# A chunked encoder layer with a mixture of experts: adaLN scales of two chunks on VectorE, features of a chunk in three rounds, and the last expert's scatter block by block

## The chip, the cores and the metric

The kernel runs on one core of a Trainium2 chip. Times are microseconds (us) on the device, from the first to the last instruction of the program and the launch around it. TensorE appears in the profile as PE (its weight loads as PEld), VectorE as DVE, ScalarE as ACT, GpSimd as POOL; SyncE (SP) issues nearly all loads. What is measured is the median of several executions.

## The reference, cut to what matters

One layer, 256 tokens, width 2048, all in float32. Every matrix product of the mixer is done on TensorE as three products of a high and a low part.

```python
mod = c_act @ w_ada[l] + b_ada[l]                 # 2048 x 12288
sh1, sc1, g1, sh2, sc2, g2 = split(mod, 6)
h = rms_norm(x, g_mix[l]) * (1 + sc1) + sh1       # "scale" sc1 and "shift" sh1 of the mixer
y = token_mixer(h, w_in[l], ...)                  # z = h @ w_in, 2048 x 4616; gMLP, pooling, attention; @ w_out
x = x + g1 * y
h = rms_norm(x, g_ffn[l]) * (1 + sc2) + sh2
x = x + g2 * moe_ffn(h, ...)                      # router, 16 experts of 2048 x 1024, top 2 of one group of 4
```

## The kernel before

The program is one long hand-written order; no scheduler moves anything. `h @ w_in` is done in five **chunks** of features (`CHUNKS`: 256, 256, 512, 512, 512 of the 2048), called chunk 0 to chunk 4 here. A chunk's `h` needs its shift (section 0 of `w_ada`) and its scale (section 1), which are themselves sums over the 2048 rows of `w_ada`; they are computed while the chunk ahead is multiplied. Chunks 0 and 1 have small pieces, chunks 2 to 4 nine **pieces** of 512 columns each.

A piece is four steps. Each step's `prep` casts a 128 x 512 tile of weights to its high part on ScalarE (line 175) and subtracts to get the low part (line 176, `whl`) on the engine that `WSPLIT` names: for chunks 2 to 4 one step of four on VectorE and three on GpSimd. Its `run` issues six matmuls into two PSUM banks (`pm`). After the fourth step `put` (line 460) adds both banks into `z` on VectorE. There are three such banks, so a piece's second bank is the first bank of the piece ahead: its fourth matmul waits for the first of the two adds of `put`.

`step` keeps a queue, `todo`, of steps whose `prep` has been issued: new ones go in at one end, and `run_first` takes the oldest out when the weights in the queue exceed `LOOK`. `then` puts a small job in the same queue. So the order on every engine is fixed by this queue and by the strings in `PLAN`: an `n` there is one `w_ada` tile for the next chunk (four row blocks of 128 x 512), a digit joins a finished shift or scale to `mod`, `h` is `make_h` of the next chunk.

A `w_ada` tile is worked in one of two ways. `ada_parts` multiplies its four row blocks on TensorE (`ada<-ring,cact`); at the end the sums are copied by ScalarE (`r`, line 314) and transposed. `sum_parts` does the same on VectorE: four multiply-and-adds into a PSUM bank (`ada`, line 297), the last of the sixteen into `ga` in SBUF, which TensorE then sums over partitions with a column of ones (`pt<-ones,ga`). `M1A` and `M1B` choose, for the shift and the scale of chunks 1 to 4: "P" is TensorE, "V" VectorE. Before, the shifts of chunks 3 and 4 are on VectorE, and all scales on TensorE.

`make_h` makes the features of a chunk: for each 128 of them VectorE scales and shifts (`hf`, line 420), ScalarE casts the high part, VectorE subtracts the low part (`hT`, line 176), and only then the next 128 follow. Eight or four more matmuls (`lgp`) use `hf`.

After the mixer come `w_out`, the router, and 15 experts in the order `ORDER`. Each loads twelve tiles of 2 MB through a ring (`load`, line 1358) whose addresses come from registers that the router's result fills. `down_stage` makes four blocks of 512 output columns: matmuls (`lbank`), a multiply by the gate on VectorE (`y`), and `late`, the scatter of the block ahead: two matmuls (`bank<-y,gt`), two adds into `xa` (line 1350) and, for the last expert only, two stores of 256 KB on ScalarE's queue (`out_dram<-xa`). The last `late` of an expert is returned and run during the next expert's loads, or, for the last one, by `pend()`. Then every engine reads `n_ov`, the number of overflow rounds, into a register, and a loop over it follows that runs no round here.

Of the kernel before, what the change touches and what calls it, by code (L numbers as in the profile page):

```python
# [11 lines left out]
F32 = mybir.dt.float32  # L12
# [4 lines left out]
OP = mybir.AluOpType  # L17
# [5 lines left out]
KD = D // 128  # L23
# [21 lines left out]
ORDER = [9, 0, 3, 10, 1, 4, 11, 2, 5, 12, 6, 7, 13, 8, 14]  # L45
# [20 lines left out]

G2, G2_MID, NG2 = [1, 2, 1, 1], 1, 8

M1A, M1B, M2A, M2B, G1 = "PPVV", "PPPP", "PPPP", "PPPP", "PVVV"
WSPLIT, WSO = ["VGVG", "VGVG", "GVGG", "GVGG", "GVGG"], "GVGG"  # L70
NORM = "GV"

# [44 lines left out]
def body(tc, x_d, prm_d, bg_d, wada_d, win_d, wout_d, egu_d, ed_d, out_d):  # L117
# [31 lines left out]

    todo = deque()  # L150

    def run_first():
        f, x, _ = todo.popleft()
        f(x) if x is not None else f()

    def step(prep, run, split=False):
        todo.append((run, prep(), split))
        while sum(0 if x is None else 1 if p else 2 for _, x, p in todo) > LOOK:
            run_first()

    def then(f):
        todo.append((f, None, False)) if todo else f()

    def flush():
        while todo:
            run_first()

    V, S, G, E = nc.vector, nc.scalar, nc.gpsimd, nc.tensor

    def mm(out, lhsT, rhs, start=True, stop=True):  # L170
        E.matmul(out, lhsT=lhsT, rhs=rhs, start=start, stop=stop, skip_group_check=True)  # L171


    def split(hi, lo, src, eng=None):
        S.copy(hi, src)  # L175
        (eng or V).tensor_tensor(lo, src, hi.bitcast(F32), op=OP.subtract)  # L176
# [65 lines left out]
    def pt():  # L242
        tbanks.rotate(-1)
        return tbanks[-1]
# [3 lines left out]
    cact = cst.tile([128, KD], F32, name="cact")  # L248
# [3 lines left out]
    def ada_load(sec, k0, nk, g):  # L252
        n = 128 * nk
        w = ring()
        load_tile(w, wada_d, ADA[sec, k0, g])
        return w.rearrange("p (k n) -> p k n", n=n)
# [23 lines left out]
    def sum_parts(sec, k0, nk, after, acc, eng, tile_of, bias=None):  # L280
        r = 16 // nk
        ng = KD // r
        P = accs[acc][:, :128 * nk]
        buf = []

        def one(g):
            def prep():
                return ada_load(sec, k0, nk, g)

            def run(w):  # L290
                for j in range(r):
                    k = r * g + j
                    ck = cact[:, k:k + 1]
                    if k == 0:
                        eng.tensor_scalar(P, w[:, j, :], ck, None, op0=OP.mult)
                    elif k < KD - 1:
                        eng.scalar_tensor_tensor(P, w[:, j, :], ck, P, op0=OP.mult, op1=OP.add)
                    else:
                        a = tile_of()[:, :128 * nk]
                        eng.scalar_tensor_tensor(a, w[:, j, :], ck, P, op0=OP.mult, op1=OP.add)  # L300
                if g == ng - 1:
                    if bias is not None:
                        eng.scalar_tensor_tensor(a[0:8, :], bgt, ident[0:8, bias:bias + 1], a[0:8, :],
                                                 op0=OP.mult, op1=OP.add)
                    after(a)
            return prep, run
        return [one(g) for g in range(ng)]

# [88 lines left out]
    def hbuf(q):  # L397
        return hTs[(len(CHUNKS) - q) % 2]
# [8 lines left out]
    def make_h(q):  # L407
        k0, nk = CHUNKS[q]
        hq = hbuf(q)
        ts = []  # L410
        for c in range(nk):
            k = k0 + c
            if c % 2 == 0:
                p2 = pt()
                for j in range(4):
                    o = 128 * (c + j // 2)
                    E.transpose(p2[:, 128 * j:128 * j + 128], xn[:, j % 2, o:o + 128], ident)
            p = p2[:, 256 * (c % 2):256 * (c % 2) + 256]
            t = wk.tile([128, T], F32, name="hf", bufs=5)
            V.tensor_scalar(t, p[:, :T], mod[:, 1, k:k + 1], mod[:, 0, k:k + 1], op0=OP.mult, op1=OP.add)  # L420
            split(hq[:, 0, c, :], hq[:, 1, c, :], t)
            ts.append((k, t))

        def late():
            for k, t in ts:
                o = 32 * (k % 4)
                mm(fzp[o:o + 8, :], wfz[:, k, :], t, start=k < 4, stop=k >= KD - 4)
        todo.insert(6, (late, None, False)) if todo else late()
# [691 lines left out]
    for h in range(2):  # L1120
        V.tensor_scalar(oneh[:, h, :], io512, sl2[:, 0, h:h + 1], None, op0=OP.is_equal)
        V.scalar_tensor_tensor(oneh[:, h, :], io512, sl2[:, 1, h:h + 1], oneh[:, h, :].bitcast(F32),
                               op0=OP.is_equal, op1=OP.add)
# [80 lines left out]
    def wide():  # L1204
        wide_ring.rotate(-1)
        return wide_ring[-1]
# [114 lines left out]
    def down_stage(w, hid, gt, load, done=None):  # L1321


        nt = 128 // w
        lhs = hid_T(w, hid)
        late = None
        for b in range(4):
            P = lbank()
            c0 = 512 * b
            t = wide()  # L1330
            load(t, ed_d, b)
            v = t.rearrange("p (k n) -> p k n", k=8)
            for kk in range(8):
                j = kk % nt
                if w == 128:
                    hl = split_piece(v[:, kk, :])
                    mm3(P, *lhs(kk), hl[:, 0, :], hl[:, 1, :], kk == 0, kk == 7)
                    continue
                mm(P[w * j:w * j + w, :], lhs(kk), v[:, kk, :], start=kk < nt, stop=kk >= 8 - nt)
            y = mo.tile([128, 512], F32, name="y")  # L1340
            V.tensor_tensor(y, P, g2w[:, c0:c0 + 512], op=OP.mult)  # L1341
            if late is not None:
                late()

            def late(y=y, c0=c0):
                for h in range(2):
                    p = bank()
                    mm(p, gt[:, 128 * h:128 * h + 128], y)
                    a = xa[:, h, c0:c0 + 512]
                    V.tensor_tensor(a, a, p, op=OP.add)  # L1350
                    if done is not None:
                        done(h, c0)
        return late

    def make_load(e):
        def load(t, flat, i):
            n = 128 * 2 * RINGW
            nc.sync.dma_start(t, flat[ds(e, 1), n * i:n * i + n].rearrange("a (p m) -> p (a m)", p=128))
        return load

    def reg(i, engines, hi, why):
        return nc.values_load(irow[0:1, i:i + 1], engines=engines, min_val=0, max_val=hi,
                              skip_runtime_bounds_check_because=why)

    why = "computed on the chip within these bounds"
    pend = None
# [21 lines left out]
    xr = tokens(ORDER[0])  # L1388
    for i, r in enumerate(ORDER):
        w = CAPS[r]  # L1390
        load = make_load(reg(r, [SP], NE - 1, why))
        gts = []
        if pend is not None:
            fill.append(pend)
        fill.insert(1, lambda: gts.append(onehot_T(w, lambda h: posR[:, h, r:r + 1], lambda h: gatR[:, h, r:r + 1])))
        hid = up_stage(w, xr, load)
        if i + 1 < len(ORDER):
            xr = tokens(ORDER[i + 1])
        pend = down_stage(w, hid, gts[0], load, store if r == ORDER[-1] else None)
    pend()  # L1400


    n_ov = reg(48, list(mybir.ALL_ENGINES), 16, why)
    for s in (s_mo, s_psB, s_psL):
        s.close()
    with tc.For_i(0, n_ov, 1) as i, ExitStack() as inner:
        mo = inner.enter_context(tc.tile_pool(name="mo2", bufs=1))
        psL = inner.enter_context(tc.tile_pool(name="psL2", bufs=6, space=PSUM))
        psB = inner.enter_context(tc.tile_pool(name="psB2", bufs=2, space=PSUM))
        e = nc.values_load(irow[0:1, ds(i + 64, 1)], engines=[SP], min_val=0, max_val=NE - 1,  # L1410
                           skip_runtime_bounds_check_because=why)
        s0 = nc.values_load(irow[0:1, ds(i + 80, 1)], engines=[DVE], min_val=0, max_val=384,
                            skip_runtime_bounds_check_because=why)
        pg = mo.tile([128, 4], F32, name="pg")
        for h in range(2):
            V.tensor_copy(pg[:, h:h + 1], posO[:, h, ds(i, 1)])
            V.tensor_copy(pg[:, 2 + h:3 + h], gatO[:, h, ds(i, 1)])
        load = make_load(e)
        xr = tokens_of(128, s0)
        gt = onehot_T(128, lambda h: pg[:, h:h + 1], lambda h: pg[:, 2 + h:3 + h])  # L1420
        hid = up_stage(128, xr, load)
        down_stage(128, hid, gt, load, store)()

    for s in (s_pl, s_pg2, s_ring2, s_ring, s_cst, root):
        s.close()
# [43 lines left out]
```

## Time and profile before

| what | us |
|---|---|
| median of 3 executions (lowest, highest) | 1412.74 (1409.59, 1419.79) |
| the profiled execution's own time | 1414.28 |
| its span, first to last instruction | 1412.5 |
| PE busy | 1207.9 (86%) |
| DVE busy | 592.7 (42%) |
| ACT busy | 363.4 (26%) |
| POOL busy | 216.9 (15%) |

The shares are averages over stages with different limits: in the first third the engines wait for one another, in the last two thirds the DMA engines are never idle. So they are read only by stretch. In a timeline a row is a run of like instructions on one engine; what stands in brackets is how long that engine was idle ahead of the row and whose work it waited for.

### The profile page before, as it was taken

To read this page: it belongs to the slowest core of one execution; us is meant where nothing else is said; L and a number is where in the kernel's file an instruction comes from. 1 tells how busy PE (TensorE), PEld (TensorE's weight loads), DVE (VectorE), ACT (ScalarE), POOL (GpSimd) and SP (SyncE) were. 2 spreads that over 40 slices of the span, in tenths; PEclk is the share of its full clock that TensorE was granted. 3 is DMA by queue.
4 is the path that set the end of the run, shared out by engine and by line. 5 is a ranking of instruction groups with operands and counts; after the bars stand their busy time and mean duration, and the time that the engine had idled before them with its cause. 6 is when DMAs were issued, how large, how long until landed. Compare 5 with 4: busy or idle time off the path is not lost.

```text
span 1412.5 us, 17042 instructions
## 1 busy us (share of the span) xinstructions
PE 1207.9 (86%) x6646; PEld 627.1 (44%) x6646; DVE 592.7 (42%) x1121; ACT 363.4 (26%) x661; POOL 216.9 (15%) x170
## 2 busy tenths in 40 slices
PE   5989999999999887989869999688885888868865
PEld 2656766665676353763327643222232222322221
DVE  4356454655884735981238832122030221302112
ACT  4633434535443332860007720000000000000000
POOL 1335545422675000000000000000000000000000
PEclk9999999999999898999989999899997999969997
DMA  9887795899989789999999989999999999999996
GB/s 390 348 347 291 291 360 209 322 359 341 374 336 369 285 366 428 427 379 370 427 427 426 416 315 428 426 428 427 426 427 426 428 426 427 426 426 429 425 425 263
DMA packets 49222, 539.14 MB, mean 382 GB/s; under 512 B 5472, under 2 KB 5600, under 8 KB 7024
## 3 DMA queue, kind: packets, MB, share of 16 engines
q1 hardware_dynamic: 47664, 534.79, 92.4%
q10 hardware_dynamic: 1472, 3.19, 0.6%
q8 instruction: 55, 0.90, 0.3%
q14 instruction: 31, 0.25, 0.0%
HBM read 535.86 MB, written 2.10 MB: 381 GB/s over the span
## 4 chain that ended last, share of the span: by engine, by line
PE 51%; DMA 35%; issue 4%; DVE 4%; ACT 2%; POOL 2%; SPq 0%; DVEq 0%; POOLq 0%; ACTq 0%
PE lbank L171 23%; PE pm L171 16%; DMA ring<-in_e_down_dram 15%; DMA ring<-in_e_gu_dram 14%; PE ada L171 5%; PE bank L171 4%; DMA ringl<-in_e_down_dram 2%; POOL whl L176 2%; DMA ringl<-in_e_gu_dram 2%; PE pt L171 1%; DMA ringm<-in_e_gu_dram 1%; DMA ring<-in_w_ada_dram 1%; DVE el L176 0%; ACT whl L175 0%; DMA bgt<-in_bg_dram 0%
## 5 line engine op out<-in xcount | busy, mean ns | idle before, releaser
L171 PE MATMUL pm<-whl,hT 128*128 128x512 f32 x1056 | 281.3, 403 | 13.0 <-DVE whl L176 6.1
L171 PEld LDWEIGHTS pm<-whl,hT 128*128 128x128 f32 x1056 | 198.7, 192 | 79.2 <-issue 11.9
L171 PE MATMUL lbank<-ring,xr 128*32 128x256 f32 (+1 forms) x1216 | 155.8, 494 | 42.9 <-DMA ring<-in_e_gu_dram 42.3
L176 POOL TENSOR_TENSOR whl<-ring,whl 128x512 fp32r<-128x512 f32 x116 | 160.8, 1408 | 181.8 <-ACT whl L175 177.5
L171 PE MATMUL bank<-y,gt 128*128 128x512 f32 x240 | 118.9, 618 | 0.0
L171 PEld LDWEIGHTS lbank<-ring,xr 128*32 128x32 f32 (+1 forms) x1216 | 55.9, 127 | 136.6 <-issue 70.0
L1350 DVE TENSOR_TENSOR xa<-xa,bank 128x512 f32<-128x512 f32 x120 | 82.5, 688 | 72.5 <-PE bank L171 72.5
L175 ACT CAST whl<-ring 128x512 fp32r<-128x512 f32 x164 | 94.6, 621 | 59.8 <-PE pm L171 46.5
L171 PE MATMUL lbank<-ringl,xr 128*32 128x256 f32 (+1 forms) x608 | 80.9, 516 | 31.7 <-DMA ringl<-in_e_gu_dram 31.7
L171 PE MATMUL lbank<-ring,hidT 128*64 128x512 f32 (+1 forms) x416 | 83.6, 703 | 28.3 <-DVE hidT L1309 16.5
L1341 DVE TENSOR_TENSOR y<-lbank,g2w 128x512 f32<-128x512 f32 x60 | 41.5, 692 | 156.8 <-PE lbank L171 156.8
L171 PE MATMUL lbank<-ringm,xr 128*32 128x256 f32 (+1 forms) x608 | 81.8, 520 | 21.2 <-DMA ringm<-in_e_gu_dram 21.2
L171 PE MATMUL lbank<-el,xs 128*128 128x512 f32 x384 | 91.1, 395 | 6.2 <-ACT el L175 4.1
L1291 DVE TENSOR_TENSOR hid<-hid,lbank 128x512 f32<-128x512 f32 x11 | 7.6, 688 | 202.4 <-PE lbank L171 202.2
L1237 ACT COPY gt<-bank 128x256 f32<-128x256 f32 x15 | 5.6, 372 | 337.1 <-PE bank L1235 337.1
L171 PEld LDWEIGHTS lbank<-el,xs 128*128 128x128 f32 x384 | 71.3, 188 | 26.1 <-ACT el L175 6.3
L460 DVE TENSOR_TENSOR z<-z,pm 128x512 f32<-128x512 f32 x72 | 49.1, 688 | 71.3 <-PE pm L171 71.1
L171 PE MATMUL lbank<-ringl,hidT 128*64 128x512 f32 (+1 forms) x416 | 74.2, 598 | 4.6 <-DMA ringl<-in_e_down_dram 4.6
L171 PE MATMUL ada<-ring,cact 128*1 128x512 f32 (+1 forms) x536 | 63.8, 575 | 16.3 <-DMA ring<-in_w_ada_dram 13.1
L171 PEld LDWEIGHTS bank<-y,gt 128*128 128x128 f32 x240 | 41.6, 191 | 72.7 <-issue 70.3
L1286 DVE TENSOR_TENSOR hid<-hid,lbank 128x256 f32<-128x256 f32 x6 | 2.5, 422 | 163.2 <-PE lbank L171 139.4
L175 ACT CAST el<-ring 128x512 fp32r<-128x512 f32 x96 | 57.4, 622 | 50.0 <-DMA ring<-in_e_gu_dram 42.9
(391 smaller groups left out, 1234.3 us busy)
## 6 DMA issues: line engine op xcount, KB each, us to landing
ring<-in_e_gu_dram SPq DMA_DIRECT2D x60, 2048.0 KB, 24.6
ring<-in_w_ada_dram SPq DMA_DIRECT2D x81, 1024.0 KB, 7.2
ringm<-in_e_gu_dram SPq DMA_DIRECT2D x30, 2048.0 KB, 25.4
ringl<-in_e_gu_dram SPq DMA_DIRECT2D x30, 2048.0 KB, 25.0
ring<-in_e_down_dram SPq DMA_DIRECT2D x30, 2048.0 KB, 25.3
ringl<-in_e_down_dram SPq DMA_DIRECT2D x30, 2048.0 KB, 25.7
ring<-in_w_in_dram SPq DMA_DIRECT2D x28, 1024.0 KB, 6.9
ring<-in_w_out_dram SPq DMA_DIRECT2D x12, 1024.0 KB, 8.4
```

The source lines that it names most:

```text
L171: E.matmul(out, lhsT=lhsT, rhs=rhs, start=start, stop=stop, skip_group_check=True)
L175: S.copy(hi, src)
L176: (eng or V).tensor_tensor(lo, src, hi.bitcast(F32), op=OP.subtract)
L460: V.tensor_tensor(dst, dst, P[h], op=OP.add)
L1237: S.copy(gt, p[:, :256])
L1286: V.tensor_tensor(hid[:, :256], hid[:, :256], P[1][:, :256], op=OP.mult)
L1291: V.tensor_tensor(hid[:, o], hid[:, o], P[2 * b + 1], op=OP.mult)
L1341: V.tensor_tensor(y, P, g2w[:, c0:c0 + 512], op=OP.mult)
L1350: V.tensor_tensor(a, a, p, op=OP.add)
```

## The change

Four edits. **Scales on VectorE**: `M1B` becomes "PPVV", so that the scales of chunks 3 and 4 (worked during chunks 2 and 3) go the way of the shifts. **Sums in twos**: a tile's first two multiply-and-adds are issued at its turn, the other two go into a second queue, `rest`, which is emptied after the next step's matmuls or ahead of the next job that is no step. **Three rounds**: `make_h` issues all `hf` of a chunk, then all casts, then all subtractions. **Last expert**: `late` of each block follows its own `y` at once, and `n_ov` is read ahead of the last expert.

```diff
-M1A, M1B, M2A, M2B, G1 = "PPVV", "PPPP", "PPPP", "PPPP", "PVVV"
+M1A, M1B, M2A, M2B, G1 = "PPVV", "PPVV", "PPPP", "PPPP", "PVVV"
...
+    rest = deque()
+
     def run_first():
-        f, x, _ = todo.popleft()
+        f, x, is_split = todo.popleft()
+        if not is_split:
+            drain()
         f(x) if x is not None else f()
+        if is_split:
+            drain()
+
+    def drain():
+        while rest:
+            rest.popleft()()
...
             def run(w):
                 for j in range(r):
...
+                    if 2 * j < r:
+                        add(w[:, j, :], r * g + j)
+                    else:
+                        rest.append(lambda wj=w[:, j, :], k=r * g + j: add(wj, k))
...
             V.tensor_scalar(t, p[:, :T], mod[:, 1, k:k + 1], mod[:, 0, k:k + 1], op0=OP.mult, op1=OP.add)
-            split(hq[:, 0, c, :], hq[:, 1, c, :], t)
             ts.append((k, t))
+        for c in range(nk):
+            S.copy(hq[:, 0, c, :], ts[c][1])
+        for c in range(nk):
+            V.tensor_tensor(hq[:, 1, c, :], ts[c][1], hq[:, 0, c, :].bitcast(F32), op=OP.subtract)
...
                     if done is not None:
                         done(h, c0)
+
+            if done is not None:
+                late()
+                late = None
         return late
...
+        if r == ORDER[-1]:
+            n_ov = reg(48, list(mybir.ALL_ENGINES), 16, why)
...
-    pend()
-
-
-    n_ov = reg(48, list(mybir.ALL_ENGINES), 16, why)
```

VectorE's rows at the entry of chunk 2, `make_h` between the scale's `mod` and the `put` of the last piece of chunk 1. Before:

```order
L342 SCALAR_TENSOR_TENSOR mod<-mod,prm_69 128x4
L420 TENSOR_SCALAR hf<-pt_122,mod 128x256
L176 TENSOR_TENSOR hT_133<-hf,hT_133 128x256
L420 TENSOR_SCALAR hf<-pt_122,mod 128x256
L176 TENSOR_TENSOR hT_133<-hf,hT_133 128x256
L420 TENSOR_SCALAR hf<-pt_123,mod 128x256
L176 TENSOR_TENSOR hT_133<-hf,hT_133 128x256
L420 TENSOR_SCALAR hf<-pt_123,mod 128x256
L176 TENSOR_TENSOR hT_133<-hf,hT_133 128x256
L460 TENSOR_TENSOR z<-z,pm_120 128x512
L460 TENSOR_TENSOR z<-z,pm_121 128x512
```

Now, on the same engine at the same place:

```order
L362 SCALAR_TENSOR_TENSOR mod<-mod,prm_69 128x4
L440 TENSOR_SCALAR hf<-pt_122,mod 128x256 x2
L440 TENSOR_SCALAR hf<-pt_123,mod 128x256 x2
L445 TENSOR_TENSOR hT_133<-hf,hT_133 128x256 x4
L483 TENSOR_TENSOR z<-z,pm_120 128x512
L483 TENSOR_TENSOR z<-z,pm_121 128x512
```

The four `hf` no longer alternate with the four subtractions that wait for ScalarE's casts.

VectorE's rows in the middle of chunk 2, from the last tiles of the shift (`spare_141`, `ring_63`) on; `whl` is a step's low part, `ring_64` and `ring_65` hold scale tiles where `cact` stands beside them. Before:

```order
L297 SCALAR_TENSOR_TENSOR ada_113<-spare_141,cact,ada_113 128x512 x4
L176 TENSOR_TENSOR whl<-ring_63,whl 128x512
L297 SCALAR_TENSOR_TENSOR ada_113<-ring_63,cact,ada_113 128x512 x3
L300 SCALAR_TENSOR_TENSOR ga<-ring_63,cact,ada_113 128x512
L460 TENSOR_TENSOR z<-z,pm_119 128x512
L460 TENSOR_TENSOR z<-z,pm_120 128x512
L176 TENSOR_TENSOR whl<-ring_65,whl 128x512
L176 TENSOR_TENSOR whl<-spare_140,whl 128x512
L460 TENSOR_TENSOR z<-z,pm_121 128x512
L460 TENSOR_TENSOR z<-z,pm_119 128x512
L337 TENSOR_TENSOR mod<-pt_122,prm_69 128x4
```

Now, on the same engine at the same place:

```order
L311 SCALAR_TENSOR_TENSOR ada_113<-spare_141,cact,ada_113 128x512 x2
L192 TENSOR_TENSOR whl<-ring_63,whl 128x512
L311 SCALAR_TENSOR_TENSOR ada_113<-spare_141,cact,ada_113 128x512 x2
L311 SCALAR_TENSOR_TENSOR ada_113<-ring_63,cact,ada_113 128x512 x3
L314 SCALAR_TENSOR_TENSOR ga<-ring_63,cact,ada_113 128x512
L483 TENSOR_TENSOR z<-z,pm_119 128x512
L483 TENSOR_TENSOR z<-z,pm_120 128x512
L309 TENSOR_SCALAR ada_113<-ring_64,cact 128x512
L311 SCALAR_TENSOR_TENSOR ada_113<-ring_64,cact,ada_113 128x512
L192 TENSOR_TENSOR whl<-ring_65,whl 128x512
L311 SCALAR_TENSOR_TENSOR ada_113<-ring_64,cact,ada_113 128x512 x6
L192 TENSOR_TENSOR whl<-spare_140,whl 128x512
```

The first `whl` moves two sums earlier; two sums of the scale stand ahead of the second, and six between the second and the third (the row of six takes in those of the next tile).

TensorE's rows at the end, from the last expert's first output block on. Before:

```order
L171 MATMUL lbank<-ring_63,hidT 32x512 x8
L171 MATMUL lbank<-ring_64,hidT 32x512 x8
L171 MATMUL bank<-y,gt 128x512 x2
L171 MATMUL lbank<-ringl_3884,hidT 32x512 x8
L171 MATMUL bank<-y,gt 128x512 x2
L171 MATMUL lbank<-ringl_3885,hidT 32x512 x8
L171 MATMUL bank<-y,gt 128x512 x4
L1362 TENSOR_LOAD irow
L1406 COMPARE_AND_BRANCH
```

Now, on the same engine at the same place:

```order
L187 MATMUL lbank<-ring_63,hidT 32x512 x8
L187 MATMUL bank<-y,gt 128x512 x2
L187 MATMUL lbank<-ring_64,hidT 32x512 x8
L187 MATMUL bank<-y,gt 128x512 x2
L187 MATMUL lbank<-ringl_3878,hidT 32x512 x8
L187 MATMUL bank<-y,gt 128x512 x2
L187 MATMUL lbank<-ringl_3879,hidT 32x512 x8
L187 MATMUL bank<-y,gt 128x512 x2
L1433 COMPARE_AND_BRANCH
```

Two scatter matmuls instead of four follow the last block, and the register load (`TENSOR_LOAD irow`) is gone from there.

## Rows read from the trace of the kernel before

**Rows 1.** Stretches: PE, PEld, DVE, ACT, POOL busy, granted clock, DMA share, GB/s.

```profile
100.00:150.00 50.00, 45.05 (x207) 32.88 (x208) 27.16 (x41) 19.30 (x33) 26.52 (x20) 0.93 0.75 291
...
900.00:1000.00 100.00, 82.83 (x378) 25.76 (x372) 21.36 (x40) 1.72 (x4) 0.00 (x0) 0.97 1.01 426
```

**Rows 2.** Chain of waits in order of time: start, us, what; features of chunk 0.

```profile
22.74 0.56 DVE hf L420
...
23.75 0.43 DVE hT L176
24.18 0.47 DVE hf L420
24.67 0.41 ACT hT L175
25.07 0.53 ACT whl L175
```

**Rows 3.** Timeline of TensorE at the entries of chunks 1 and 2.

```profile
61.37 3.69 PE L171 MATMUL pm<-whl,hT 128*128 128x512 f32 x15 [1.17 <-ACT z L458]
...
102.35 6.29 PE L171 MATMUL pm<-whl,hT 128*128 128x512 f32 x15 [3.40 <-DVE z L460]
```

**Rows 4.** Timeline of VectorE at the entry of chunk 2, first and last row.

```profile
96.21 0.54 DVE L420 TENSOR_SCALAR hf<-pt,mod 128x256 f32<-128x256 f32 x1
...
101.62 1.28 DVE L460 TENSOR_TENSOR z<-z,pm 128x512 f32<-128x512 f32 x2
```

**Rows 5.** Busy time of the first microseconds of chunk 2, columns as in rows 1.

```profile
102.00:105.00 3.00, 2.65 (x6) 2.15 (x7) 1.67 (x3) 1.43 (x3) 3.00 (x3) 0.50 0.32 57
```

**Rows 6.** Timeline of VectorE in the middle of chunk 2.

```profile
121.02 1.37 DVE L460 TENSOR_TENSOR z<-z,pm 128x512 f32<-128x512 f32 x2 [1.03 <-PE pm L171]
122.31 3.12 DVE L297 SCALAR_TENSOR_TENSOR ada<-spare,cact,ada 128x512 f32<-128x512 f32 x4
125.34 0.68 DVE L176 TENSOR_TENSOR whl<-ring,whl 128x512 fp32r<-128x512 f32 x1
125.94 2.33 DVE L297 SCALAR_TENSOR_TENSOR ada<-ring,cact,ada 128x512 f32<-128x512 f32 x3
```

**Rows 7.** Timeline of TensorE in chunks 2 and 3 and at the entries of chunks 3 and 4.

```profile
126.08 3.93 PE L171 MATMUL pm<-whl,hT 128*128 128x512 f32 x16 [2.60 <-DVE whl L176]
129.94 1.90 PE L171 MATMUL ada<-ring,cact 128*1 128x512 f32 x16
...
138.44 1.05 PE L171 MATMUL pt<-ones,ga 128*128 128x1 f32 x8
...
152.59 0.66 PE L327 MATMUL pt<-ident,r 128*128 128x128 f32 x4
...
188.63 5.56 PE L171 MATMUL pm<-whl,hT 128*128 128x512 f32 x16 [2.60 <-DVE whl L176]
...
230.97 7.00 PE L171 MATMUL pm<-whl,hT 128*128 128x512 f32 x28 [0.63 <-POOL whl L176]
```

**Rows 8.** Timeline of TensorE at the entry of chunk 3.

```profile
166.35 4.04 PE L171 MATMUL pm<-whl,hT 128*128 128x512 f32 x15 [0.24 <-POOL whl L176]
```

**Rows 9.** Timeline of the last expert's output.

```profile
1387.07 2.84 PE L171 MATMUL lbank<-ring,hidT 128*32 128x512 f32 x16 [2.97 <-DMA ring<-in_e_down_dram]
...
1392.45 11.54 ACTq L1319 DMA_DIRECT2D out_dram<-xa  x8
...
1397.15 1.93 PE L171 MATMUL lbank<-ringl,hidT 128*32 128x512 f32 x16 [0.83 <-DMA ringl<-in_e_down_dram]
...
1399.01 3.89 PE L171 MATMUL bank<-y,gt 128*128 128x512 f32 x8
...
1399.14 0.69 DVE L1341 TENSOR_TENSOR y<-lbank,g2w 128x512 f32<-128x512 f32 x1 [2.10 <-PE lbank L171]
```

**Rows 10.** Instructions of the register read and of the loop's branches, TensorE's queue.

```profile
L1362 PEldq TENSOR_LOAD <-irow x1: 703/703/703, 1401.8 to 1401.8; - x1
...
L1406 PEldq COMPARE_BRANCH  x3: 97/310/4230, 1402.7 to 1411.3; - x3
```

More of the change, by code (lines that the diff above doesn't have):

```diff
@@ L161, in then @@
     def then(f):
-        todo.append((f, None, False)) if todo else f()
+        if todo:
+            todo.append((f, None, False))
+        else:
+            drain()
+            f()
     def flush():
@@ L166, in flush @@
             run_first()
+        drain()
     V, S, G, E = nc.vector, nc.scalar, nc.gpsimd, nc.tensor
@@ L288, in prep, with add @@
                 return ada_load(sec, k0, nk, g)
[L290 to L301, printed above, removed]
+            def add(wj, k):
+                ck = cact[:, k:k + 1]
+                if k == 0:
+                    eng.tensor_scalar(P, wj, ck, None, op0=OP.mult)
+                elif k < KD - 1:
+                    eng.scalar_tensor_tensor(P, wj, ck, P, op0=OP.mult, op1=OP.add)
+                else:
+                    a = tile_of()[:, :128 * nk]
+                    eng.scalar_tensor_tensor(a, wj, ck, P, op0=OP.mult, op1=OP.add)
                     if bias is not None:
@@ L305, in run @@
                     after(a)
+            def run(w):
+                for j in range(r):
+                    if 2 * j < r:
+                        add(w[:, j, :], r * g + j)
+                    else:
+                        rest.append(lambda wj=w[:, j, :], k=r * g + j: add(wj, k))
             return prep, run
@@ L1421, in body @@
         hid = up_stage(128, xr, load)
-        down_stage(128, hid, gt, load, store)()
+        down_stage(128, hid, gt, load, store)
     for s in (s_pl, s_pg2, s_ring2, s_ring, s_cst, root):
```

## The prediction

> **What bounds the kernel now.** I read the stretches first. Up to the router TensorE is nearly full and the DMA engines are not; behind it the weights of the experts fill the DMA engines, at 426 GB/s, whatever TensorE does [rows 1]. The experts' loads cannot start before the router has given their addresses, so what is won ahead of it moves the whole stream forward, and the full amount arrives at the end. Three of the four edits lie ahead of it, the last expert's at its end.
>
> Inside the first part I read the chain of waits, then the timelines for TensorE's gaps. The chain runs through the features of a chunk one by one [rows 2]; TensorE stands still at every entry of a chunk [rows 3, 7, 8], longest, 3.40 us, ahead of chunk 2, and it waits 2.60 us for one `whl` of VectorE in the middle of chunks 2 and 3 [rows 7]. These gaps and TensorE's own work are what can be won.
>
> **Three rounds, chunks 0 and 1.** Two features cost, before ScalarE's next cast may begin, 25.07 - 22.74 = 2.33 us: scale, cast, low part, scale, cast, each waiting for the one ahead [rows 2]. In rounds the chain is `hf`, `hf`, one cast: 0.47 + 0.56 + 0.41 = 1.44. That is 0.9 earlier. TensorE's next work is the cast that follows, so chunk 0 starts 0.9 earlier. At chunk 1 TensorE waited 1.17 us for ScalarE's copy of the last piece, which queues behind the same two features [rows 3]; 0.9 of it goes. Sum **-1.8**; bounds 0 (another wait stands behind each, the stretch being near the DMA limit) and -2.1, the full 1.17 and 0.9.
>
> **Three rounds, chunk 2.** Four features take VectorE from 96.21 to 101.62, 5.41 us [rows 4], and only then comes the `put` whose first half TensorE waits for [rows 3]. In rounds: 0.56 + 3 x 0.47 for `hf`, 4 x 0.43 for the low parts, 3.69; the last cast ends 0.45 after the last `hf`, hidden by the first low part. 5.41 - 3.69 = **-1.7** from the gap of 3.40. [...]
>
> **Chunks 3 and 4, entries.** There TensorE has most of a piece left to work while the features are made, and waits at the end 0.24 and 0.63 us for a low part of GpSimd whose cast queues behind them [rows 7, 8]. With the casts 1.7 earlier both go: **-0.9**, bound 0.
>
> **Scales on VectorE.** Off TensorE go four tiles in each of two chunks: two tiles take 1.90 [rows 7], four 3.8. The four transposes (0.66) become sums by ones (1.05 for the same number) [rows 7], +0.4. ScalarE loses a copy. VectorE gains 16 multiply-and-adds a chunk, 0.78 each [rows 6], 12.5 us. Over the whole chunk it has room: 32 sums 25.0, nine `put` 12.3, nine `whl` 6.1, features 3.7, in all 47 of the 64 us from one entry to the next [rows 3, 8]. But the order decides, since four tiles fall on two neighbouring pieces, so I walk it, with the durations of rows 6 and 7.
>
> `put` at 121.02, two sums, `whl` from 123.87: TensorE, idle from 123.48, goes on at 124.6, a gap of 1.1 in place of 2.60. This is what the twos give. 16 matmuls end the piece at 128.5. VectorE has six sums first and comes to `put` at 129.15; its first half ends at 129.85, while TensorE could use the bank at 129.2: a gap of 0.7. `put` ends at 130.45; two sums, then the next `whl`, ready at 132.7; TensorE needed it at 131.1: 1.65. Then six sums and a `whl` to 137.9, and `put` is late again, by 0.45, the shift's sums by ones, 1.05, having covered some of it. From there one tile falls on each piece, 1.4 + 3.1 + 0.7 against a piece of some 5.7, and nothing is late. Gaps in all 3.9 against 2.60, +1.3. A chunk gains 3.8 - 0.4 - 1.3 = 2.1; two chunks **-4.2**. Bounds: 0, if late `put`s cost all that the tiles give, and -8.0, if only 2.0 of the gaps stay in each (2 x (3.8 - 0.4 + 2.60 - 2.0)).
>
> The ring slots of the scale tiles come free when VectorE has read them, 3 to 5 us later than TensorE had. The loads that wait for those slots are for pieces some three further on, about 17 us, which hides it; if that cover went, the price would be those 3 to 5 us once a chunk. In chunk 3 the gap of 2.60 was followed by 16 matmuls in 5.56, not 3.93 [rows 7]: a fall of the clock worth 1.6. The same gap in chunk 2 had none, so I leave it out of the sum and in the range. [...]
>
> **The tail.** Before, the last block is followed by the scatter of the block ahead, then its own: eight matmul passes, 3.89, from 1399.01 [rows 9]. Now only its own four, half of that, 1.95, but they wait for `y`, to 1399.83 and some 0.1: end 1401.9 in place of 1402.9, -1.0. TensorE then had its register read, 0.70, in front of the branch; that is done long before now, where TensorE waits some 3 us for each load [rows 9, 10], -0.7. Its branch of 4.23 us and what follows stay [rows 10]; I take them to end the program in both. Against this, the stores of the first two blocks come earlier, ahead of the last loads' landing. Before, one block's did: the two loads from 1387.07 to 1397.15 took 10.1 us, where 2 x 2.1 MB at 426 GB/s make 9.8, so a block's stores cost 0.3. One more block: +0.3. [...] Sum **-1.4**, bounds -2.0 and 0.
>
> **Sum.** -1.8 - 1.7 - 2.6 - 0.9 - 4.2 - 1.4 = **-12.6**. The profiled execution, 1414.28, would be 1401.7. It lies 1.54 above the median, 1412.74; the forecast is 1400.1, 0.9% faster.
>
> **Rivals.**
> (a) *VectorE's late `put`s eat the tiles.* The walk is tight by tenths at three places, and each gap may bring the clock down as in chunk 3. For it: 2.60 us already came from four sums ahead of a `whl`. Against: the twos put fewer in front. The 4.2 go, 1.6 for one new fall come: 1400.1 + 5.8 = 1406.
> (b) *The clock stays low at chunk 2's entry.* For: a gap of 1.7 remains. Against: full speed after 2.60. 1400.1 + 2.6 = 1403.
> (c) *More is won*: the fall in chunk 3 does not come either (1.6) and only 2.0 of the gaps stay in each chunk (3.8): 1394.7.
> (d) *Slower than before*: VectorE becomes what TensorE waits for throughout chunks 2 and 3. Then all 32 added sums show, 25.0, for 7.6 of TensorE's, and 17.4 replaces the gain of 4.2: 1400.1 + 21.6 = 1421.7. It decides from where VectorE's work for a piece exceeds a piece of TensorE on average, not only on the two pieces with two tiles; 47 of 64 us speaks against it.
> (e) *The reorder is hidden*, the chain being replaced at each entry by GpSimd's low parts, which had stood still there: 1.8 + 1.7 + 2.6 + 0.9 are lost, 1407.
>
> **How the numbers follow.** Chances: forecast 0.5, (a) 0.2, (b) 0.1, (c) 0.12, (d) 0.04, (e) 0.04. Another run of three may give a median some 2 us off. The range goes from (c) to a little past (a): 1394.5 to 1408.5, and leaves out (d) and the ends of the others. 1% is about what a measurement can tell from no change: 1398.6 and 1426.9. Below 1398.6 lie (c) and a third of the forecast's spread, 0.3; above 1426.9 only the far end of (d), 0.02; within, 0.68.
>
> **What would show it.** Right: the low parts of `make_h` stand in one row of four, TensorE's gap ahead of chunk 2 is below 2 us and its next 15 matmuls take below 4; in the middle of chunk 2 there are three or four gaps of 0.5 to 1.7 in place of one of 2.60; the first load of the experts is issued some 11 us earlier; TensorE's branch of 4 us begins 1.7 earlier against the last landing. Wrong: gaps named after VectorE's `z` or `whl` at every piece of chunks 2 and 3 (a, d), a clock of 0.50 at the entry of chunk 2 (b), or the same start of the experts' loads with all entries shorter, which would mean a limit between chunk 4 and the router that I do not see.

## The result, and the profile after

| | before | after |
|---|---|---|
| median of 7 executions each | 1412.30 | 1399.97 |
| ratio, 95% interval | | 0.9905 [0.9883, 0.9926] |
| the profiled execution | 1414.28 | 1398.13 |
| its span | 1412.5 | 1396.4 |
| PE, DVE busy | 1207.9, 592.7 | 1195.6, 616.5 |

One of the seven executions after took 5053 us; it is left out of the ratio, and without it the median is 1399.05. The time falls by 0.95%, some 13 us.

TensorE's timeline after, at the entries of chunks 0, 1 and 2, in the middle of chunks 2 and 3, at the last transposes of `make_h` in both, and from the entries of chunks 3 and 4 on (columns as in [rows 3]):

```profile
24.09 6.02 PE L187 MATMUL pm<-whl,hT 128*128 128x512 f32 x24 [0.36 <-ACT whl L191]
...
57.52 3.69 PE L187 MATMUL pm<-whl,hT 128*128 128x512 f32 x15 [0.27 <-ACT z L481]
...
96.28 3.73 PE L187 MATMUL pm<-whl,hT 128*128 128x512 f32 x15 [0.87 <-DVE z L483]
...
115.89 4.62 PE L187 MATMUL pm<-whl,hT 128*128 128x512 f32 x19 [1.05 <-DVE whl L192]
121.10 1.42 PE L187 MATMUL pm<-whl,hT 128*128 128x512 f32 x5 [0.59 <-DVE z L483]
124.71 5.51 PE L187 MATMUL pm<-whl,hT 128*128 128x512 f32 x16 [2.19 <-DVE whl L192]
...
149.35 1.03 PE L437 MATMUL pt<-ident,xn 128*128 128x128 f32 x8
...
156.16 19.79 PE L187 MATMUL pm<-whl,hT 128*128 128x512 f32 x86
...
185.95 5.51 PE L187 MATMUL pm<-whl,hT 128*128 128x512 f32 x16 [2.18 <-DVE whl L192]
...
210.79 1.03 PE L437 MATMUL pt<-ident,xn 128*128 128x128 f32 x8
...
224.62 1.04 PE L187 MATMUL ada<-ring,cact 128*1 128x512 f32 x8
```

The last transposes and the entries of chunks 3 and 4 before:

```profile
158.57 1.03 PE L417 MATMUL pt<-ident,xn 128*128 128x128 f32 x8
...
166.35 19.68 PE L171 MATMUL pm<-whl,hT 128*128 128x512 f32 x84 [0.24 <-POOL whl L176]
...
222.72 1.03 PE L417 MATMUL pt<-ident,xn 128*128 128x128 f32 x8
...
237.90 1.04 PE L171 MATMUL ada<-ring,cact 128*1 128x512 f32 x8
```

The entries are short now: 0.27 in place of 1.17 and 0.87 in place of 3.40 [rows 3], and the 15 matmuls behind the second take 3.73 at a granted clock of 1.00 (96.28 to 100.01), where they took 6.29 [rows 3] and the clock was 0.50 in their first 3 us [rows 5]. The one gap of 2.60 [rows 7] has become three, 1.05, 0.59 and 2.19. Behind the last, 16 matmuls took 5.51 and not 3.93, in both chunks; before, it was so in chunk 3 only, with 5.56 [rows 7].

VectorE's timeline after, at the entry of chunk 2 and at the low part that ends the gap of 2.19:

```profile
92.39 1.90 DVE L440 TENSOR_SCALAR hf<-pt,mod 128x256 f32<-128x256 f32 x4
94.20 1.42 DVE L445 TENSOR_TENSOR hT<-hf,hT 128x256 fp32r<-128x256 f32 x4
95.54 1.28 DVE L483 TENSOR_TENSOR z<-z,pm 128x512 f32<-128x512 f32 x2
...
123.01 1.65 DVE L192 TENSOR_TENSOR whl<-ring,whl 128x512 fp32r<-128x512 f32 x1
```

GpSimd's timeline at the same moment, and the busy times of the stretch behind it (columns as in [rows 1]):

```profile
122.85 1.26 POOL L192 TENSOR_TENSOR whl<-spare,whl 128x512 fp32r<-128x512 f32 x1 [1.71 <-ACT whl L191]
```

```profile
124.70:130.00 5.30, 5.29 (x16) 4.22 (x17) 5.12 (x8) 1.24 (x2) 1.99 (x2) 0.68 0.98 369
```

The four features take 95.54 - 92.39 = 3.15 us to the `put`, where they took 5.41 [rows 4]. The low part at 123.01 took 1.65 where one takes 0.68 [rows 6]: GpSimd had begun a subtraction 0.16 us earlier, it ended at 124.11, and VectorE's ended 0.55 later. The granted clock in the stretch behind it was 0.68; behind the gap of 2.60 in chunk 2 it was 1.00 before (126.08 to 130.01).

The first load of an expert, in SyncE's queue, in the kernel before and after:

```profile
482.29 0.35 SPq L1358 DMA_DIRECT2D ring<-in_e_gu_dram  x1
```

```profile
469.56 0.35 SPq L1385 DMA_DIRECT2D ring<-in_e_gu_dram  x1
```

The end of the kernel after: stores, the last landing and the last scatter in the timeline, then the loop's branches in TensorE's queue (as in [rows 10]):

```profile
1374.39 16.45 ACTq L1342 DMA_DIRECT2D out_dram<-xa  x8
...
1385.02 1.92 PE L187 MATMUL lbank<-ringl,hidT 128*32 128x512 f32 x16 [0.79 <-DMA ringl<-in_e_down_dram]
1387.76 1.98 PE L187 MATMUL bank<-y,gt 128*128 128x512 f32 x4 [0.81 <-DVE y L1364]
```

```profile
L1433 PEldq EVENT_SEMAPHORE  x9: 51/51/51, 1389.8 to 1394.8; - x9
L1433 PEldq COMPARE_BRANCH  x3: 101/196/3996, 1387.9 to 1394.9; - x3
```

The loads begin 12.7 us earlier, and the last one lands 1397.15 - 1385.02 = 12.1 earlier: the start is passed on to the end almost whole, although the DMA engines are not without idle time behind it (before, their share was 0.92 from 500 to 550 us and 0.91 from 600 to 650). From the last landing to the last matmul's end it is 4.7 us now, 5.75 before [rows 9]. From there to the end of the span it was 1412.5 - 1402.9 = 9.6 us and is 1396.4 - 1389.7 = 6.7. Together 12.1 + 1.0 + 2.9 = 16.0, against 16.1 of the spans. The last 2.9 was in no term of the prediction. The two profiled executions lie 2.0 above and 1.8 below their medians, so what is read from them adds up to more than the 12.3 between the medians.

### The profile page after: what moved, and what is told of

Read it like the earlier page. It is cut to its first block, busy times and chain, and to the rows that moved or that the text cites. A ratio compares the mean times of both kernels' runs of the same rounds, so it can differ in the third digit from the quotient of the medians.

```text
span 1396.4 us, 16964 instructions
## 1 busy us (share of the span) xinstructions
PE 1195.6 (86%) x6590; PEld 624.7 (45%) x6590; DVE 616.5 (44%) x1151; ACT 363.0 (26%) x659; POOL 219.4 (16%) x170
## 4 chain that ended last, share of the span: by engine, by line
PE 50%; DMA 38%; DVE 5%; issue 3%; ACT 2%; POOL 1%; SPq 0%; DVEq 0%; POOLq 0%; ACTq 0%
PE lbank L187 22%; DMA ring<-in_e_gu_dram 19%; PE pm L187 16%; DMA ring<-in_e_down_dram 15%; PE ada L187 5%; PE bank L187 3%; DMA ringl<-in_e_down_dram 2%; PE pt L187 1%; DMA ring<-in_w_ada_dram 1%; POOL whl L192 1%; DVE ada L311 1%; ACT whl L191 1%; DMA spare<-in_w_in_dram 0%; DVE el L192 0%; DMA ring<-in_w_in_dram 0%
## 5 line engine op out<-in xcount | busy, mean ns | idle before, releaser
L187 PE MATMUL pm<-whl,hT 128*128 128x512 f32 x1056 | 278.0, 400 | 10.2 <-DVE whl L192 6.6
L187 PE MATMUL lbank<-ring,xr 128*32 128x256 f32 (+1 forms) x1216 | 152.7, 482 | 39.9 <-DMA ring<-in_e_gu_dram 39.3
L187 PE MATMUL lbank<-ring,hidT 128*64 128x512 f32 (+1 forms) x416 | 82.2, 689 | 25.6 <-DVE hidT L1332 16.1
L187 PE MATMUL ada<-ring,cact 128*1 128x512 f32 (+1 forms) x488 | 57.3, 570 | 16.5 <-DMA ring<-in_w_ada_dram 13.3
```

## The experiments

**The parts apart.** Four kernels, each with some edits of the change alone.

Three rounds only:

```diff
-            split(hq[:, 0, c, :], hq[:, 1, c, :], t)
             ts.append((k, t))
+        for c in range(nk):
+            S.copy(hq[:, 0, c, :], ts[c][1])
+        for c in range(nk):
+            V.tensor_tensor(hq[:, 1, c, :], ts[c][1], hq[:, 0, c, :].bitcast(F32), op=OP.subtract)
```

> The kernel before with the three rounds alone. Theory of the features' chain (the gain is mostly at the entries of the chunks): the entries of chunks 0 and 1 give 2 to 4 us, that of chunk 2 gives 2.5 plus 2.6 for the clock that no longer falls, those of chunks 3 and 4 give 1 to 2, in all 8 to 10 us off 1412.3, 1402 to 1404; the gap ahead of chunk 2 is 0.9 us and its next 15 matmuls take 3.7. Rival, that the entries are hidden behind GpSimd's low parts and the gain comes from the scales: less than 4 us.

Measured: 1404.34, ratio 0.9944 [0.9921, 0.9967], some 8 us less.

Scales on VectorE with the sums in twos (`M1B` and `rest`, `drain`):

```diff
-M1A, M1B, M2A, M2B, G1 = "PPVV", "PPPP", "PPPP", "PPPP", "PVVV"
+M1A, M1B, M2A, M2B, G1 = "PPVV", "PPVV", "PPPP", "PPPP", "PVVV"
...
+                    if 2 * j < r:
+                        add(w[:, j, :], r * g + j)
+                    else:
+                        rest.append(lambda wj=w[:, j, :], k=r * g + j: add(wj, k))
```

> The kernel before with the scales of chunks 3 and 4 on VectorE and the sums in twos, no other edit. Features' chain: chunk 2 gives about 0.6 and chunk 3 about 2.2 us, since VectorE's late adds and a low part held up by GpSimd give back half of what leaves TensorE: 3 us off, 1409. The prediction's walk: 4.2 off, 1408. Rival, that the scales are the larger part of the gain: 8 us off or more, 1404.

Measured: 1407.18, ratio 0.9960 [0.9944, 0.9976], 5.6 less.

The scales alone, in fours as before (the line of `M1B` only):

> The kernel before with the scales of chunks 3 and 4 on VectorE, the sums left in fours. If the twos are what makes the move pay: the gap of 2.6 us in each chunk stays, the next low part stands behind four sums instead of two and comes 1.5 us later, so 3 to 5 us slower than the scales in twos, 1411 to 1414, no gain over before. Rival, that the order of the sums does not matter: the same as in twos within 1 us.

Measured: 1411.23, ratio 0.9989 [0.9971, 1.0008]. TensorE's timeline of this kernel in the middle of chunk 2:

```profile
121.54 7.36 PE L171 MATMUL pm<-whl,hT 128*128 128x512 f32 x24 [2.60 <-DVE whl L176]
...
131.48 5.53 PE L171 MATMUL pm<-whl,hT 128*128 128x512 f32 x16 [2.59 <-DVE whl L176]
```

Two gaps of 2.6 stand where one stood [rows 7]. The second eats most of the 3.4 that leave TensorE, and the clock fell behind both: 24 matmuls took 7.36, where 24 later in the chunk take 5.70, and 16 took 5.53, where they took 3.93 before [rows 7].

The tail alone (`late` with each block, `n_ov` ahead of the last expert; the move of `n_ov` isn't shown):

```diff
+            if done is not None:
+                late()
+                late = None
...
-    pend()
```

> The kernel before with the two edits of the last expert alone (scatter with each block, register read ahead of it). The prediction: 1.4 us off, 1411. From the trace of the changed kernel: the program ends 6.7 us behind TensorE's last matmul in place of 9.6, so 3 to 4 us off, 1408.5 to 1409. Rival, that those 3 us belong to the moment and not to the edit: 0.5 to 1 off, and a stretch behind the last matmul that is again 9 to 10 us in its profile.

Measured: 1411.70, ratio 0.9999 [0.9980, 1.0019]. Its timeline from the landing of the last tile in `ringm`, four loads ahead of the end, its branches, and the same landing before and after the whole change:

```profile
1376.33 3.54 PE L171 MATMUL lbank<-ringm,xr 128*32 128x256 f32 x32 [2.98 <-DMA ringm<-in_e_gu_dram]
...
1392.70 1.93 PE L171 MATMUL lbank<-ringl,hidT 128*32 128x512 f32 x16 [1.82 <-DMA ringl<-in_e_down_dram]
...
1398.21 1.92 PE L171 MATMUL lbank<-ringl,hidT 128*32 128x512 f32 x16 [0.79 <-DMA ringl<-in_e_down_dram]
```

```profile
L1410 PEldq COMPARE_BRANCH  x3: 97/310/4086, 1401.0 to 1410.7; - x3
```

```profile
1377.18 3.20 PE L171 MATMUL lbank<-ringm,xr 128*32 128x256 f32 x32 [2.98 <-DMA ringm<-in_e_gu_dram]
```

```profile
1364.61 3.55 PE L187 MATMUL lbank<-ringm,xr 128*32 128x256 f32 x32 [4.29 <-DMA ringm<-in_e_gu_dram]
```

The last four loads take 1398.21 - 1376.33 = 21.9 us here, 1397.15 - 1377.18 = 20.0 before [rows 9] and 1385.02 - 1364.61 = 20.4 after. In the seven profiles without the tail's edits they take 19.7 to 20.35, in the six others with them 20.3 to 20.4. So the earlier stores cost some 0.4 to 0.6 in most profiles, which leaves half of the 1.0 that the shorter scatter gives, and 1.9 in this one, which takes back all of it; why this one lost more is open. The longest branch takes 4.09, 4.23 before [rows 10]. By the three ratios (rounds, scales in twos, tail) 7.9 + 5.6 + 0.1 = 13.6 us of 1412, and the whole change 13.4: the parts add up, within intervals of 2 to 3 us to either side of each.

**Twos alone**, scales still on TensorE (the second piece of the diff of the scales in twos without `M1B`).

> The kernel before with the sums in twos alone, scales still on TensorE. Theory: the wait of 2.60 us in the middle of chunks 2 and 3 comes from four sums that stand ahead of one low part on VectorE; with two ahead it becomes about 1.1 in both chunks, and the fall of the clock behind it in chunk 3 (1.6) goes: 3 to 4.6 us less, 1408.3 to 1410, and most of what the scales on VectorE with the sums in twos gave (5.7) is this. Rival: the twos only help where the scales are on VectorE; the wait moves to the put behind the postponed sums: 1412 to 1413.

Measured: 1407.30, ratio 0.9980 [0.9961, 0.9999], 2.8 less. TensorE's timeline in chunk 2:

```profile
122.06 3.93 PE L187 MATMUL pm<-whl,hT 128*128 128x512 f32 x16 [1.33 <-DVE whl L192]
...
126.68 1.90 PE L187 MATMUL ada<-ring,cact 128*1 128x512 f32 x16 [0.69 <-DVE ga L314]
```

The gap of 2.60 is split into 1.33 and 0.69, and no fall came: 16 matmuls took 3.93. By the ratios, half of what the scales in twos gave is this.

**Is it the two neighbouring pieces with two tiles?** The changed kernel with the tiles over seven pieces:

```diff
-    ["n", "n", "nn", "nn", "n0", "n", "m1", "hm", ""],
+    ["n", "n", "n", "nn", "n0", "n", "nm1", "hm", ""],
```

> The changed kernel with the eight tiles of a chunk spread over seven pieces (1, 1, 1, 2, 1, 1, 1) in place of six (1, 1, 2, 2, 1, 1). Theory: what ate the scales' gain in chunks 2 and 3 is the two neighbouring pieces with two tiles: late put 0.59 and the low part of 1.65 us that ends a wait of 2.19, with the clock's fall behind it (1.6 for 16 matmuls). With one such piece alone 0.6 to 2.8 of the gaps and the fall go, in each chunk: 3 to 7 us less, 1393 to 1397. Rival: the low part of 1.65 comes from GpSimd's subtraction beside it, whatever the number of tiles, and only moves to another piece: 1399 to 1401.

Measured: 1403.67, ratio 0.9937 [0.9913, 0.9962], not faster than the change, and the 1393 to 1397 that were expected did not come. TensorE's timeline in chunk 2:

```profile
122.46 3.96 PE L187 MATMUL pm<-whl,hT 128*128 128x512 f32 x16 [1.02 <-DVE whl L192]
...
128.32 10.61 PE L187 MATMUL pm<-whl,hT 128*128 128x512 f32 x45 [0.31 <-DVE z L483]
...
143.21 1.87 PE L187 MATMUL pt<-ones,ga 128*128 128x1 f32 x8 [3.31 <-DVE ga L314]
144.94 7.89 PE L187 MATMUL pm<-whl,hT 128*128 128x512 f32 x24
```

The theory holds for the middle, where 1.3 is left of 3.8. But the last tile now stands right ahead of the sums by ones, TensorE waits 3.31 for it, and the clock falls there (24 matmuls in 7.89, where the 24 at that place take 5.70 in the kernel with all low parts on GpSimd, which comes next).

**Low parts on GpSimd alone**, in the changed kernel and in the kernel before:

```diff
-WSPLIT, WSO = ["VGVG", "VGVG", "GVGG", "GVGG", "GVGG"], "GVGG"
+WSPLIT, WSO = ["VGVG", "VGVG", "GGGG", "GGGG", "GVGG"], "GVGG"
```

> The changed kernel with all low parts of the weights of chunks 2 and 3 on GpSimd; VectorE makes none there. Theory: TensorE's waits in the middle of chunks 2 and 3 (1.05 and 2.19 us, both for a low part of VectorE that queues behind its sums) go, GpSimd needing 4 x 1.29 = 5.2 us for a piece of 5.7; the put's 0.6 stays, perhaps grows: 2 x 3.2 and the clock's fall, 1.6 each, less: 1391 to 1396. Rival: GpSimd has too little room (its subtraction takes 1.7 us where it runs beside a low part or a subtraction of VectorE) and is late at every piece, some 0.5 us each: 1404 to 1409.

> The kernel before with the low parts of the weights of chunks 2 and 3 on GpSimd alone, nothing else changed. Theory: TensorE's waits of 2.60 us for a low part of VectorE in the middle of chunks 2 and 3 go, and the clock's fall behind one of them (1.6): 6.8 less, 1404 to 1407; the step from the changed kernel to the one with this added (7 to 9 us) is then mostly this wait, in its new form, and not the scales. Rival: the wait in chunks 2 and 3 of before is set by the sums' put as well, which stands behind the same four sums, and little goes: 1410 to 1412.

Measured: in the changed kernel 1391.22, ratio 0.9856 [0.9832, 0.9879], clearly faster than the change; in the kernel before 1409.24, ratio 0.9994 [0.9978, 1.0010], nothing that can be told. TensorE's timelines, with the scales on VectorE and then without:

```profile
120.58 5.07 PE L187 MATMUL pm<-whl,hT 128*128 128x512 f32 x21 [1.46 <-DVE z L483]
...
127.97 10.49 PE L187 MATMUL pm<-whl,hT 128*128 128x512 f32 x45 [0.74 <-DVE z L483]
...
145.81 1.03 PE L437 MATMUL pt<-ident,xn 128*128 128x128 f32 x8
...
203.40 1.03 PE L437 MATMUL pt<-ident,xn 128*128 128x128 f32 x8
```

```profile
126.58 1.90 PE L171 MATMUL ada<-ring,cact 128*1 128x512 f32 x16 [1.54 <-DVE ga L300]
```

With the change the two waits for a low part are gone, 2.20 of 3.83 is left, for `put`, and the clock does not fall (1.00 from 160 to 225, 0.97 there in the changed kernel): chunk 3 takes 203.40 - 145.81 = 57.6 from transposes to transposes, 61.4 after, 64.15 before (158.57 to 222.72 there). In the kernel before the wait shrank to 1.54 only, now for the last of the sums: my 6.8, 1404 to 1407, was too much, since two wait for the same four sums.

**The same with seven pieces**, and the sums by ones a piece later:

```diff
-    ["n", "n", "nn", "nn", "n0", "n", "m1", "hm", ""],
+    ["n", "n", "n", "nn", "n0", "n", "nm", "1hm", ""],
```

> The changed kernel with the low parts of chunks 2 and 3 on GpSimd alone, and besides the eight tiles of a chunk over seven pieces (1, 1, 1, 2, 1, 1, 1), the scale's sums by ones one piece later, so that they wait for no tile just issued. Theory: what is left of TensorE's waits there with GpSimd alone (1.46 and 0.74 us a chunk, both for a late put) comes from the two neighbouring pieces with two tiles each; with one such piece about 0.7 stays, and no wait for the last sum (3.31 us in the variant with seven pieces and the low parts on both engines) comes: 2 to 3 us below the kernel with GpSimd alone, 1387.5 to 1389.5. Rival: a chunk's end then waits for the scale, which is ready a piece later, by 1 to 3 us at the entry of the next chunk, and the gain is lost: 1391 to 1394.

Measured: 1389.08, ratio 0.9831 [0.9803, 0.9860], the fastest kernel here, 24 us less than before by the ratio, though its interval meets that of the kernel with the low parts on GpSimd alone (0.9856). TensorE's timeline, the gap of chunk 2 and that of chunk 3:

```profile
126.97 10.49 PE L187 MATMUL pm<-whl,hT 128*128 128x512 f32 x45 [0.55 <-DVE z L483]
...
182.56 10.49 PE L187 MATMUL pm<-whl,hT 128*128 128x512 f32 x45 [0.55 <-DVE z L483]
```

One gap of 0.55 a chunk is left, and no wait at the entries came of it.

**The stretch behind the last matmul.** It was long (9.0 to 9.6 us) in four kernels whose TensorE program has 6646 matmuls by the profile (before, rounds, tail, twos), and short (6.7 to 7.1) in the three of 6590 run till then (the change, and both with the scales on VectorE alone). So matmuls of one column were added at the start, where TensorE waits for its first loads: 56 and 28 to the changed kernel, 28 to the one before.

```diff
+    for _ in range(28):
+        mm(tbanks[0][0:1, :1], ident[:, :1], ident[:, :1])
```

> The changed kernel with 56 matmuls of one column added at the start, while TensorE stands idle for its first loads, so that TensorE's program has as many matmuls as before; nothing else is changed and no result uses them. Theory: the stretch behind the last matmul (9.6 us before, 9.5 with the three rounds alone, 9.0 with the tail's edits alone, but 6.7 to 7.1 in the three kernels with the scales on VectorE) depends on where in TensorE's program the loop's branch stands; it goes back to 9 to 9.6 and the time to 1402.3 to 1402.9. Rival: it depends on the engines' work at the end, which is the same: 6.7, and 1400.0 (1399 to 1400.5).

> The changed kernel with 28 matmuls of one column added at the start, while TensorE waits for its first loads; the profile counts each twice, so TensorE's program is now as long as before (6646 records, 6590 in the changed kernel). Theory: the stretch behind the last matmul depends on where in TensorE's program the loop's branch stands; with the length of before it is 9.0 to 9.6 us again (all four kernels of 6646 records had that), the time 2.5 us above the changed kernel's: 1402 to 1403. Rival: it belongs to the scales on VectorE, whatever the length: 6.4 to 7.1, the time as the changed kernel's.

> The kernel before with the same 28 matmuls added at the start: 6702 records on TensorE, as many as the changed kernel with 56 had, whose last stretch was 6.8 us. Theory of the branch's place: 6.4 to 7.1 in place of 9.6, the time 2.5 below before: 1408 to 1410.5. Rival: scales on TensorE keep it long: 9.0 to 9.6, and 1411 to 1413.

Measured, in that order: 1398.79, ratio 0.9917 [0.9891, 0.9943]; 1400.57, 0.9918 [0.9897, 0.9938]; 1408.77, 0.9975 [0.9956, 0.9994]. With 56 the profile counts 6702 matmuls, 56 more than before, so that run did not make the lengths equal; its last stretch stayed at 6.8. The branches of TensorE's queue in the other two, the changed kernel with 28 and the kernel before with 28:

```profile
L1435 PEldq COMPARE_BRANCH  x3: 97/310/4046, 1390.0 to 1399.5; - x3
```

```profile
L1408 PEldq COMPARE_BRANCH  x3: 97/193/4033, 1401.7 to 1407.1; - x3
```

From the first branch to the last it is 9.5 us in the changed kernel of 6646 matmuls, 7.0 without the padding; and 5.4 in the kernel before at 6702, 8.6 without it [rows 10]. The last stretch becomes 1400.7 - 1391.9 = 8.8 and 1408.4 - 1401.9 = 6.5. In all fourteen profiles the six programs of 6646 matmuls have the long stretch, 8.8 to 9.65 us, and the eight of 6590 or 6702 the short one, 6.4 to 7.1. So in these fourteen the 3 us go with the length of TensorE's program, not with the work in it.

They are not in the branch itself, which takes 4.0 to 4.35 us in all fourteen, but in a standstill behind it. TensorE's semaphore instructions behind the branch, before (in two stretches) and after:

```profile
L1406 PEldq EVENT_SEMAPHORE  x4: 51/51/51, 1407.4 to 1407.7; - x4
...
L1406 PEldq EVENT_SEMAPHORE  x4: 51/51/51, 1410.9 to 1411.2; - x4
```

```profile
L1433 PEldq EVENT_SEMAPHORE  x8: 51/51/51, 1394.0 to 1394.8; - x8
```

After, the eight follow one another; before, nothing starts from 1407.7 to 1410.9. Each of the six long programs stands still there once, for 2.5 to 3.2 us, and none of the eight short ones.

The measured times show it less well than the profiles. The kernel before became 3.5 us [0.8, 6.2] faster by 28 idle matmuls. But the changed kernel with 28, whose stretch is long, and with 56, whose stretch is short, have the same ratio, 0.9918 and 0.9917, both slower than without by some 0.0013; the intervals can't tell 2.5 us there.

## Why the prediction was right, point by point

1400.1 was forecast and 1399.97 came. The mechanism of the rounds was right, but that the number fits so well is luck. By the profiles the scales gave some 1.8 us less than their term and the tail 0.8 less; the entries of chunks 3 and 4 gave 1.3 more, the start of chunk 0 1.9 more, and the very end, which had no term, 2.9.

- **Three rounds, chunks 0 and 1, -1.8.** Right. Chunk 1 starts 3.85 earlier, which holds the 0.9 of the gap (1.17 to 0.27) and the 0.9 of the chain; of the rest, 1.4 is a fall of the clock at chunk 0 that I had not seen (24 matmuls in 7.40 at a granted clock of 0.77 before, in 6.02 at 1.00 after), and 0.5 was there before any edit acts (chunk 0's last `mod` starts at 21.79, 22.28 before). The fall stood in five of the seven profiles without the rounds and in none of the seven with them, so it is probably theirs too. The bound of 0 took the stretch to be near the DMA limit; the DMA share was 1.01, at 418 GB/s, from 20 to 60 us before, and the gain came all the same. The rounds alone gave 7.9 [4.7, 11.2], where their terms, 1.8 + 1.7 + 2.6 + 0.9, make 7.0.
- **Three rounds, chunk 2, -1.7 and -2.6.** Right in kind. The four features took 3.15 and not 3.69, 2.3 less than before. The gap fell by 2.5, but 0.3 of that only moved into the row ahead of it, whose 15 matmuls took 3.94 in place of 3.67: from the start of chunk 1 to that of chunk 2 it is 96.28 - 57.52 = 38.8 us in place of 41.0, 2.2 won. That the clock would be up behind a shorter gap, on which the 2.6 rests, was my estimate: no run shows a gap below which it must be. In its place the runs show these 15 matmuls in 6.29 before, at a granted clock of 0.56 over all of them (102.35 to 108.64), and in 3.73 after, at 1.00. The clock stayed up in every other kernel with the rounds too, with 3.69 to 3.73 for the 15. The 2.6 is no fixed price: without the rounds the clock fell behind this gap in five of seven profiles (15 matmuls in 6.20 with the scales in twos, 3.70 with the scales in fours).
- **Entries of chunks 3 and 4, -0.9.** Right in kind, too small. Both gaps are gone, and so are shorter waits within the rows beside them that the timeline does not set apart. From the last transposes to the end of the row of 84 or 86 matmuls chunk 3's entry takes 175.95 - 149.35 = 26.6 us in place of 27.5, and from the transposes to the next `ada` chunk 4's takes 13.8 in place of 15.2: 0.9 and 1.35, together 2.2. The kernel with the rounds alone shows the same 26.6 and 13.8.
- **Scales on VectorE, -4.2.** Mis-sized: -2.4, from the timelines. Chunk 2 gained 0.6 behind its first 15 matmuls (49.9 to 49.3 us to the transposes), chunk 3 1.8 (2.7 less the entry's 0.9), where 2.1 each were forecast. The walk's gaps, 1.1 + 0.7 + 1.65 + 0.45 = 3.9, came as 1.05 + 0.59 + 2.19 = 3.8. But the gap that I had as 1.65 was 2.19, in which VectorE's low part took 1.65 and not 0.68 beside GpSimd's, and behind it came a fall of the clock in chunk 2, 1.6 for 16 matmuls, that the gap of 2.60 there had not brought before. It came in the two padded kernels of the change too (16 matmuls in 5.33 and 6.71), but not with the scales in twos alone (3.92), with nearly the same gaps. This is rival (a) for one chunk of two. In the kernel with the scales in twos alone chunk 2 took 48.7, so of the 1.5 that are missing in chunk 2 the fall is 0.6, and 0.9 are missing without it. Put beside the twos alone, -2.8, the scales' -5.6 holds the last stretch's 2.5 to 3; what is left for taking the scales off TensorE is little, by the timelines of the two kernels 1.1 us in chunks 2 and 3 together (49.4 to 48.7 and 61.7 to 61.3), until the low parts leave VectorE.
- **The tail, -1.4.** Too much: -0.6 by the profile. The scatter's -1.0 was right, and the stores cost some 0.4 where 0.3 was worked out. The register read's -0.7 was wrong: before, it ran while the last matmuls were still under way, and the long branch came behind these in any case: it started at 1403.1, and the last matmul ended at 1402.9. I expected the branch 1.7 us earlier against the last landing; it came 1.0 earlier. Alone the tail gave nothing.
- **"Its branch of 4.23 us and what follows stay"** failed: the branch took 4.0, but what follows it shrank, and with it the stretch behind the last matmul, by 2.9. The prediction took this part of the end as the same in both, and in the fourteen profiles it goes with the length of TensorE's program: 8.8 to 9.65 us at 6646 matmuls, 6.4 to 7.1 at 6590 and 6702.
- **Rivals.** (b), (c), (d) and (e) did not come: a granted clock of 1.00 at chunk 2's entry, falls in chunks 2 and 3, no wait at every piece, and loads 12.7 us earlier where 11.2 was worked out.

## What to carry to other kernels

Work moved from a full engine to one with room on average pays only if what the full engine waits for does not queue behind it: here the scales' sums gave about 1 us until the low parts left VectorE, and the low parts' move by itself gave nothing that could be told, but the two together, with the other edits, gave 20 us. By the timelines of chunks 2 and 3 the scales and twos gave 5.2 us once the low parts were gone (48.6 to 45.8 and 60.9 to 57.6, less 0.9 for the rounds). How much of this the twos would give with the scales still on TensorE was not run; the waits for the sums that were left there are one of 1.54 a chunk. Walk the two or three pieces in which the load is doubled, with the durations of operations that overlap on both engines (a low part of 1.65 here), not those of one alone (0.68). And before a few microseconds at the very end are put down to an edit, look whether the edit merely changed the length of a program that ends in a branch; here that went with 2.5 to 3.2 us.

## What the runs showed of the hardware

- In the middle of chunk 2 a low part of VectorE (`whl`) that began 0.16 behind one of GpSimd took 1.65 in place of 0.68, and it ended 0.55 behind GpSimd's end. Two operations on 128 x 4 (`mod`) were long beside GpSimd's too: in the kernel with the low parts on GpSimd alone they took 0.93 and 1.21 at the entry of chunk 2, the second until 92.29, where GpSimd's second subtraction ended at 92.27; in the changed kernel, where GpSimd had just ended (at 92.06), the second of them took 0.16. First GpSimd's and VectorE's rows of the former kernel, then VectorE's of the latter:

```profile
89.75 2.52 POOL L192 TENSOR_TENSOR whl<-ring,whl 128x512 fp32r<-128x512 f32 x2 [4.29 <-ACT whl L191]
...
90.11 0.93 DVE L361 TENSOR_TENSOR mod<-c,prm 128x4 f32<-128x4 f32 x1
91.08 1.21 DVE L362 SCALAR_TENSOR_TENSOR mod<-mod,prm 128x4 f32<-128x4 f32 x1
```

```profile
92.11 0.16 DVE L362 SCALAR_TENSOR_TENSOR mod<-mod,prm 128x4 f32<-128x4 f32 x1
```

- The branch around a loop that runs no round took TensorE 4.0 to 4.35 us in all fourteen profiles, and in the six programs of 6646 matmuls a standstill of 2.5 to 3.2 followed it, in the eight of 6590 or 6702 none. What TensorE does in the 4 us and in the standstill is not shown.
- The granted clock fell behind some gaps of 2.2 to 3.9 us and not behind others of the same size: before, behind two of 2.60, it was 1.00 for 16 matmuls in 3.93 in chunk 2 and 0.69 for 16 in 5.56 in chunk 3. In the kernels that share their work up to a gap it mostly did the same there (16 matmuls in the middle of chunk 2 in 3.92 to 3.94 before, with the tail alone and with the padding, in chunk 3 in 5.54 to 5.56 in all three). Behind the gaps of up to 1.5 in the middle of chunks 2 and 3 no row was slow in any of these traces (16 matmuls in 3.93 behind 1.33, 21 in 5.07 behind 1.46). What decides is open.
